# A matrix product in fp16 on one core: w's blocks converted two at a time, and the first group's differences made for two blocks in one operation

## The chip, the cores and the metric

The kernel runs on one core of a Trainium2 chip. The metric is the device time of one execution in microseconds (us), as the median of several runs. The engines are called by their short names: PE (TensorE, matrix products), DVE (VectorE), ACT (ScalarE), POOL (GpSimd) and SP (SyncE, whose queue issues the DMAs).

## The reference

```python
cs = np.cumsum(x, axis=1)
diff = cs - np.concatenate([zeros, cs[:, :-1, :]], axis=1)
return np.matmul(diff, w).astype(np.float32)
```

x is 8 x 2048 x 2048 and w is 2048 x 2048, both float32. The differences of the running sums are x itself, so that the kernel computes x times w, with x as 16384 rows of 2048. On the chip that is 128 tiles of 128 rows.

## The kernel before

**Products.** Four row tiles make a group: g, g+1, g+2 and g+3, of which the code calls g+2 "h". The kernel splits the 2048 contraction values and the 2048 columns in two each, so that w has four blocks B11, B12, B21, B22, and pairs of row tiles are combined in a scheme with seven products in place of eight. For that it needs four differences of w's blocks: T1 = B12 - B11, T2 = B22 - T1, T3 = B22 - B12, T4 = B21 - T2. Blocks and differences are fp16, scaled by one number for each column half of w, made from sums of absolute values (`uw`, and its reciprocal `uinv`). Row tiles are scaled too: ACT measures a tile (`weigh`), DVE makes its scale (`scale_of`, two tiny operations), POOL its unit for the way back (`unit_of`), ACT narrows it to fp16 (`narrow`), and SP issues two transposing DMAs (`turn`). Results leave PSUM scaled by the unit, by ACT (`keep`, the first part of an output) or DVE (`add`, a further part), and SP stores them (`put`).

**The storage of w.** `W_all` holds w as it was loaded, float32, in eight slots k of 4 x 1024 values. The two halves of the contraction (a) and of the columns (h) each take 1024 float32 values of a slot, 4096 bytes. A converted block takes half of that place, as two runs of 512 fp16 values with a gap of 512 after each, and the difference of the same place takes the gaps:

```python
blocks = W_all.bitcast(f16).rearrange("p k (i n j c) -> p i j k n c", i=4, j=2, c=NB)

def spare_of(i, k):
    return blocks[:, i // 2, i % 2, ds(k, 2), :, :]
```

With i from 0 to 7 these are B11, T1, B12, T2, B21, T3, B22, T4. A conversion (`block`, lines 337 to 346; DVE's form at 341, ACT's at 345) multiplies the 1024 float32 values of one slot by `uinv` and writes them in place. `spare_of(i, k)` is the view of two slots, k and k+1, of one of the eight; it is used before the change for sums inside later groups.

**The head.** The first four row tiles are multiplied plainly in bf16 while w is loaded, in two passes over w's column halves (h = 0 and 1) of 16 steps ko, eight matmuls a step in the second pass. Each step has `cast` (DVE writes the bf16 copy `wb`, line 266) and `measure` (ACT, line 272). In the second pass `bring(ko)` fetches, casts and measures step ko, and then converts one block of the first half with `turn_left(1)`, in the order B11 0 to 7, B21 0 to 7, from ko = 1. At ko = 10 it loads and measures tile 4, and DVE makes its scale. The matmuls of steps 0 to 11 go over all four rows; those of steps 12 to 15 are done row by row by `finish_row(r)`, which then copies the row's two PSUM banks out (ACT the even bank, DVE the odd, lines 331 and 333). After the last step come `greatest_of_w(1)` and `scale_of_w(1)` (the scale of the second half, with a reduction on POOL), the one block left (`turn_left(KH)`), and then the eight blocks of B12, with the rows' copies among them. `left_over` (line 457) is a product of 16 matmuls that the first pass left out; it reads B11 and B21. Then the head makes T1 (line 506), eight operations.

**The first group** (`group_plain`, tiles 4 to 7). It converts B22 (0 to 5 on ACT, 6 and 7 on DVE) and makes T2, T3 and T4 with `lessen` (line 586), one slot at a time, each ahead of the product that reads it. Products of sixteen matmuls with 512 columns (line 604) read a block k after k. Its first sums of row tiles (`total`, line 594) need the transposes of tile 5.

**What sets the order.** Each engine works in the order of the program: `after(engine, ...)` ties each operation behind the last one of its engine, and SP's DMAs likewise. Waits between engines come from the data. From the second group (`group_half`) on, the order is a list of steps written out by hand, which this change does not touch.

Of the kernel before, what the change touches and what calls it, by code (L numbers as in the profile page):

```python
# [10 lines left out]
def kernel(  # L11
# [6 lines left out]
    nc = tc.nc  # L18
    P = 128
    B, S, D = x.shape  # L20
# [4 lines left out]
    KH = KO // 2  # L25
    NH = N // 2
    NB = 512
# [4 lines left out]
    SUB = mybir.AluOpType.subtract  # L32
    MUL = mybir.AluOpType.mult
# [18 lines left out]
    W_all = const.tile([P, KH, 4 * NH], f32, name="W")  # L52
# [5 lines left out]
    B11, T1, B12, T2, B21, T3, B22, T4 = (  # L58
        [p[:, i // 2, i % 2] for p in pieces] for i in range(8)
    )  # L60
# [6 lines left out]

    def spare_of(i, k):
        return blocks[:, i // 2, i % 2, ds(k, 2), :, :]

    uw = const.tile([P, 2], f32, name="uw")
    uinv = const.tile([P, 2], f32, name="uinv")
# [9 lines left out]
    def bank(i):  # L82
        return psum.tile([P, NB], f32, name=f"b{i}")
# [3 lines left out]
    def after(engine, ask):  # L87
        if engine in last:
            with tc.issue_after(last[engine].ins):
                said = ask()  # L90
        else:
            said = ask()
        last[engine] = said[-1] if isinstance(said, tuple) else said
        return said
# [90 lines left out]
    with ExitStack() as head:  # L185
# [70 lines left out]
        def fetch(h, ko):  # L256
            wt = whole[ko % KH][:, ko // KH, h, :]
            nc.sync.dma_start(wt, w[ds(ko * P, P), ds(h * NH, NH)])
# [37 lines left out]
        def here(h, r):  # L296
            return range(1 if h == 0 and r == PLAIN - 1 else 2)
# [39 lines left out]
        def block(dst, a, h, k, engine):  # L337
            src = whole[k][:, a, h, :].rearrange("p (n c) -> p n c", c=NB)
            if engine == "dve":
                after(  # L340
                    "dve", lambda: nc.vector.tensor_scalar(dst[k], src, uinv[:, h : h + 1], None, MUL)  # L341
                )
            else:
                after(
                    "act", lambda: nc.scalar.activation(dst[k], src, COPY, scale=uinv[:, h : h + 1])
                )

        def dummies(banks):
            for i in banks:
                after(  # L350
                    "pe",
                    lambda: nc.tensor.matmul(
                        bank(i), zeros[:, :P], zeros, start=True, stop=True
                    ),
                )
# [25 lines left out]
        for ko in range(1, KO - 2):  # L381
# [3 lines left out]
            q = (ko + 1) // KQ  # L385
# [3 lines left out]
            for r in range(PLAIN):  # L389
                if turning and r in (0, PLAIN - 1):  # L390
                    a = r // 2
# [13 lines left out]
        for ko in range(AHEAD):  # L405
            measure(1, ko)
        ps = [[bank(2 * r + n) for n in here(1, r)] for r in range(PLAIN)]
        left = [(B, a, k) for a, B in enumerate((B11, B21)) for k in range(KH)]

        def turn_left(n):  # L410
            for _ in range(min(n, len(left))):
                B, a, k = left.pop(0)
                block(B, a, 0, k, "dve")

        def bring(ko):
            fetch(1, ko)
            cast(1, ko)
            measure(1, ko)
            if ko == AHEAD:
                scale_of_w(0)  # L420
            turn_left(1)
            if ko == 10:
                load(PLAIN, 0)
                load(PLAIN, 1)
                weigh(PLAIN)
                scale_of(PLAIN)
            if ko == 11:
                narrow(PLAIN)
# [18 lines left out]
        def finish_row(r):  # L447
            for ko in range(KO - KQ, KO):
                plain(1, r, ko)
            plain_out(1, r)  # L450
# [16 lines left out]
            rows = ds((PLAIN - 1) * P, P)  # L467
            after("sp", lambda: put(c, rows, ds(NB, NB), nc.sync))

        turn_left(KH)  # L470
        unit_of(PLAIN)
        turn(PLAIN)
        weigh(PLAIN + 2)
        finish_row(0)
        for k in range(KH):
            block(B12, 0, 1, k, "dve")
            if k == 1:
                scale_of(PLAIN + 2)
            if k % 2:
                if k // 2:  # L480
                    finish_row(k // 2)
        unit_of(PLAIN + 2)
        narrow(PLAIN + 2)
        there = xP.rearrange("p r k m -> p (r k m)")
# [17 lines left out]
        stores(done[:3] + done[5:])  # L502
        left_over(bank(2))

        for k in range(KH):
            after("dve", lambda: nc.vector.tensor_tensor(T1[k], B12[k], B11[k], SUB))


    class Part:
# [64 lines left out]
    def in_twos(t):  # L574
        return t if len(t.shape) == 4 else t.rearrange("p (a b) n -> p a b n", b=2)
# [4 lines left out]

    def half_of(t, i):
        return in_twos(t)[:, i]

    def lessen(dst, p, q):
        for k in range(len(dst)):
            after("dve", lambda: nc.vector.tensor_tensor(dst[k], p[k], q[k], SUB))

    def less(dst, p, q):
        if len(dst.shape) == 4 or len(p.shape) == 4 or len(q.shape) == 4:
# [88 lines left out]
    def group_plain(g, X, Y, Z, V):  # L678
        h = g + 2
        lg, lh, kg = (units(t)[0] for t in (g, h, g + 1))  # L680
        ug, uh, vg = (units(t)[1] for t in (g, h, g + 1))
        A11g, A12g = parts(g)
        A11h, A12h = parts(h)
        A21g, A22g = parts(g + 1)
        A21h, A22h = parts(h + 1)
        S1g, S1h = S1
        S2g, S2h, S3g, S3h, S4g, S4h = A11g, A11h, A21g, A21h, A12g, A12h
        load(g + 4, 0)
        load(g + 4, 1)
        product(X, A11g, B11, True)  # L690
        for k in range(3):
            block(B22, 1, 1, k, "act")
        C11g = pair()
        keeps(C11g, X, lg)
        weigh(h + 1)
        for k in range(3, KH):
            block(B22, 1, 1, k, "act" if k < 6 else "dve")
        product(V, A12g, B21, True)
        product(Y, A11h, B11, True)
        lessen(T2[:1], B22[:1], T1[:1])  # L700
        adds(C11g, V, lg)
        puts(C11g, g, 0)
        lessen(T2[1:2], B22[1:2], T1[1:2])
        total(S1g, A21g, A22g, ADD)
        total(S3g, A11g, A21g, SUB)
        total(S2g, S1g, A11g, SUB)
        scale_of(h + 1)
        unit_of(h + 1)
        narrow(h + 1)
        kh, vh = units(h + 1)  # L710
        turn(h + 1)
        lessen(T2[2:], B22[2:], T1[2:])
        product(Z, A12h, B21, True)
        C11h, C22g = (
            [
                inner[:, ds(j, 2), :].rearrange("p a n -> p (a n)").bitcast(f32)
                for j in (i, i + 2)
            ]
            for i in (12, 16)
        )  # L720
        keeps(C11h, Y, lh)
        product(V, S1g, T1, True)
        keeps(C22g, V, vg)
        load(h + 4, 0)
        total(S4g, A12g, S2g, SUB)
        product(X, S2g, T2, False)
        C12g = pair()
        keeps(C12g, X, ug)
        lessen(T3, B22, B12)
        product(V, S4g, B22, False)  # L730
        total(S1h, A21h, A22h, ADD)
        total(S3h, A11h, A21h, SUB)
        total(S2h, S1h, A11h, SUB)
        weigh(g + 4)
        scale_of(g + 4)
        unit_of(g + 4)
        narrow(g + 4)
        load(h + 4, 1)
        turn(g + 4)
        load(g + 5, 0)  # L740
        load(g + 5, 1)
        product(X, S3g, T3, False)
        adds(C11h, Z, lh)
        puts(C11h, h, 0)
        del free[-2:]
        adds(C12g, V, ug)
        puts(C12g, g, 1)
        product(Y, S2h, T2, False)
        C12h = pair()
        keeps(C12h, Y, uh)  # L750
        adds(C22g, X, vg)
        puts(C22g, g + 1, 1)
        del free[-2:]
        total(S4h, A12h, S2h, SUB)
        product(Z, S1h, T1, True)
        weigh(h + 4)
        lessen(T4[:4], B21[:4], T2[:4])
        scale_of(h + 4)
        unit_of(h + 4)
        lessen(T4[4:], B21[4:], T2[4:])  # L760
        C22h = pair()
        keeps(C22h, Z, vh)
        narrow(h + 4)
        weigh(g + 5)
        product(Y, S3h, T3, False)
        in_2.first()
        in_2.fourth()
        load(h + 5, 0)
        load(h + 5, 1)
        turn(h + 4, [0])  # L770
        scale_of(g + 5)
        unit_of(g + 5)
        adds(C22h, Y, vh)
        puts(C22h, h + 1, 1)
        product(Z, S4h, B22, False)
        in_2.third()
        adds(C12h, Z, uh)
        puts(C12h, h, 1)
        narrow(g + 5)
        weigh(h + 5)  # L780
        turn(h + 4, [1])
        turn(g + 5, [0])
        product(X, A22g, T4, False)
        C21 = pair()
        keeps(C21, X, kg)
        puts(C21, g + 1, 0)
        turn(g + 5, [1])
        product(Y, A22h, T4, False)
        less(in_3.Q1, in_3.t12, in_3.t11)
        scale_of(h + 5)  # L790
        unit_of(h + 5)
        C21 = pair()
        keeps(C21, Y, kh)
        narrow(h + 5)
        in_3.second()
        less(in_1.Q1, in_1.t12, in_1.t11)
        turn(h + 5)
        load(g + 8, 0)
        load(g + 8, 1)
        puts(C21, h + 1, 0)  # L800
# [462 lines left out]
    for b in range(-early, len(groups) - late):  # L1263
        for name, ahead in ORDER:
            i = b + ahead
# [41 lines left out]
```

## Time and profile before

| | |
|---|---|
| median of 3 runs | 1451.99 us (1451.88 to 1452.24) |
| the profiled execution's own time | 1450.92 us |
| its span in the trace | 1449.10 us |
| granted clock of TensorE | 1.00 throughout |
| busy: PE, DVE, ACT, POOL | 1439.1, 1318.3, 971.7, 43.5 us |
| conversions on DVE (line 341) | 26, from 42.0 to 79.6 us, median 750 ns |
| T1 on DVE (line 506) | 8, from 74.2 to 78.4 us, median 686 ns |
| T2, T3 and T4 on DVE (line 586) | 24, from 80.3 to 108.8 us, median 686 ns |
| PE's left-over product | starts at 68.03 us |
| the first group's first product | starts at 71.48 us |

Times in the text are microseconds from the start of the span unless something else is said. A timeline row has the start, the length, the engine, the line of the kernel, the operation, what it writes and reads by the program's names, shapes, how many neighbours were merged into the row, and in brackets the idle time of the engine before it with what ended it. The chain of work that ended last is followed back from the last instruction, at each step to what released it. The durations of matmuls include the pipeline, so that the distance between starts is what counts for PE.

### The profile page before, as it was taken

To read this page: it belongs to the slowest core of one execution; us is meant where nothing else is said; L and a number is where in the kernel's file an instruction comes from. 1 tells how busy PE (TensorE), PEld (TensorE's weight loads), DVE (VectorE), ACT (ScalarE), POOL (GpSimd) and SP (SyncE) were. 2 spreads that over 40 slices of the span, in tenths; PEclk is the share of its full clock that TensorE was granted. 3 is DMA by queue.
4 is the path that set the end of the run, shared out by engine and by line. 5 is a ranking of instruction groups with operands and counts; after the bars stand their busy time and mean duration, and the time that the engine had idled before them with its cause. 6 is when DMAs were issued, how large, how long until landed. Compare 5 with 4: busy or idle time off the path is not lost.

```text
span 1449.1 us, 20194 instructions
## 1 busy us (share of the span) xinstructions
PE 1439.1 (99%) x6686; PEld 651.7 (45%) x6692; DVE 1318.3 (91%) x2309; ACT 971.7 (67%) x1473; POOL 43.5 (3%) x130
## 2 busy tenths in 40 slices
PE   8999999999999999999999999999999999999998
PEld 4444444444444444444444444444444444444443
DVE  5898899999999999999999999999999999999998
ACT  6987567766666776666666667666667766666662
POOL 0011000000000000000000000000000000000000
PEclk9999999999999999999999999999999999999999
DMA  9999788899888898888898878998878998889973
GB/s 363 371 246 294 202 232 237 234 258 246 231 220 241 243 248 243 231 234 239 248 250 232 235 232 235 263 236 237 228 234 239 253 239 235 224 244 247 254 201 126
DMA packets 378199, 351.58 MB, mean 243 GB/s; under 512 B 274800, under 2 KB 274800, under 8 KB 377968
## 3 DMA queue, kind: packets, MB, share of 16 engines
q1 hardware_dynamic: 378096, 350.31, 86.7%
q8 instruction: 52, 0.85, 0.2%
q14 instruction: 51, 0.42, 0.1%
HBM read 150.99 MB, written 134.22 MB: 197 GB/s over the span
## 4 chain that ended last, share of the span: by engine, by line
PE 93%; DMA 5%; DVE 1%; issue 0%; ACT 0%; SPq 0%; DVEq 0%; ACTq 0%
PE b L623 61%; PE b L604 31%; DMA W<-in_w_dram 4%; DMA x<-F 1%; DVE c L634 1%; PE b L303 0%; DVE x L594 0%; PE b L457 0%; DMA out_dram<-c 0%; DVE wb L266 0%; DVE W L341 0%; ACT c L631 0%; ACT F L163 0%; SPq L224 0%; DVE S L594 0%
## 5 line engine op out<-in xcount | busy, mean ns | idle before, releaser
L634 DVE SCALAR_TENSOR_TENSOR c<-b,of,c 128x512 f32<-128x512 f32 x790 | 573.6, 746 | 70.2 <-PE b L623 60.0
L604 PE MATMUL b<-W,x 128*128 128x512 f16 x2144 | 506.8, 379 | 0.2 <-DVE x L594 0.2
L631 ACT ACTIVATE c<-b,of 128x512 f32<-128x512 f32 x492 | 312.7, 680 | 223.0 <-PE b L623 117.2
L623 PE MATMUL b<-W,x 128*128 128x512 f16 x1904 | 455.0, 379 | 0.1
L163 ACT ACTIVATE F<-F,of 128x1024 f16<-128x1024 f32 x246 | 282.2, 1147 | 175.1 <-DVE of L143 172.9
L623 PEld LDWEIGHTS <-x 128*128 128x128 f16 x2500 | 244.6, 98 | 296.1 <-issue 1.9
L604 PEld LDWEIGHTS <-x 128*128 128x128 f16 x2144 | 209.7, 98 | 253.4 <-DVE x L594 0.7
L124 ACT ACTIVATE waste<-F 128x1024 uint8<-128x1024 f32 x246 | 259.3, 1054 | 8.7 <-DMA F<-in_x_dram 6.6
L623 PEld LDWEIGHTS <-inner 128*128 128x128 f16 x1644 | 160.9, 98 | 194.0 <-issue 0.2
L623 PE MATMUL b<-W,inner 128*128 128x512 f16 x940 | 241.2, 379 | 0.0
L594 DVE TENSOR_TENSOR x<-x,x 128x1024 f16<-128x1024 f16 (+1 forms) x390 | 227.2, 583 | 3.2
L623 PE MATMUL b<-flow,x 128*128 128x512 f16 x588 | 150.9, 379 | 0.1
L623 PE MATMUL b<-inner 128*128 128x512 f16 x472 | 121.1, 379 | 0.0
L947 DVE TENSOR_TENSOR flow<-W 128x2048 f16<-128x2048 f16 x88 | 107.0, 1216 | 0.0
L1040 DVE TENSOR_TENSOR b<-b,c 128x512 f32<-128x512 f32 x116 | 80.5, 694 | 13.4 <-PE b L623 13.4
L149 POOL TENSOR_SCALAR of<-uw,of 128x2 f32<-128x2 f32 x124 | 42.2, 354 | 1301.6 <-DVE of L141 719.3
L947 DVE TENSOR_TENSOR flow<-W,inner 128x2048 f16<-128x2048 f16 x58 | 70.8, 1220 | 0.0
L1033 ACT COPY c<-b 128x512 f32<-128x512 f32 x58 | 33.4, 576 | 52.1 <-PE b L623 46.6
L303 PE MATMUL b<-wb,xP 128*128 128x512 bf16 x234 | 53.5, 379 | 2.8 <-ACT wb L264 1.9
L594 DVE TENSOR_TENSOR inner<-x 128x512 f16<-128x512 f16 x117 | 49.3, 421 | 3.1 <-DMA x<-F 1.1
L1033 ACT COPY b<-b 128x512 f32<-128x512 f32 x87 | 51.2, 588 | 0.0
L594 DVE TENSOR_TENSOR inner<-x,inner 128x512 f16<-128x512 f16 x117 | 49.2, 421 | 2.0
(66 smaller groups left out, 516.6 us busy)
## 6 DMA issues: line engine op xcount, KB each, us to landing
F<-in_x_dram SPq DMA_DIRECT2D x246, 512.0 KB, 5.3
out_dram<-c SPq DMA_DIRECT2D x492, 256.0 KB, 3.1
W<-in_w_dram SPq DMA_DIRECT2D x32, 512.0 KB, 8.4
W<-in_x_dram SPq DMA_DIRECT2D x16, 256.0 KB, 7.8
x<-F SPq DMA_TRANSPOSE x246, 3.4
out_dram<-o SPq DMA_DIRECT2D x5, 256.0 KB, 7.6
out_dram<-wb SPq DMA_DIRECT2D x5, 256.0 KB, 3.5
xP<-in_x_dram SPq DMA_DIRECT2D x1, 1024.0 KB, 6.2
```

Of the source, the lines that this page charges most:

```text
L124: lambda: nc.scalar.activation(waste, where[t][i], ABS, scale=1.0 / ROW, accum_out=sums_of[t][:, i : i + 1],),
L149: after("pool", lambda: nc.gpsimd.tensor_scalar(u, uw, m, None, MUL))
L163: lambda: nc.scalar.activation(narrowed(t)[:, ds(i * NH, NH)], where[t][i], COPY, scale=s),
L303: lambda: nc.tensor.matmul(ps[r][n], xP[:, r, ko, :], wb[h, ko][:, ds(n * NB, NB)], start=(ko == 0), stop=(ko == KO - 1),),
L594: after("dve", lambda: nc.vector.tensor_tensor(dst.all, p.all, q.all, op))
L604: said = nc.tensor.matmul(to[n], a[k], b[k][:, n, :], start=(first and k == 0), stop=(k == KH - 1), skip_group_check=True,)
L623: said = nc.tensor.matmul(to, a[k], b[k], start=(first and k == 0), stop=(k == 3), skip_group_check=True)
L631: after("act", lambda: nc.scalar.activation(c, p, COPY, scale=u))
L634: after("dve", lambda: nc.vector.scalar_tensor_tensor(c, p, u, c, MUL, ADD))
L947: after("dve", lambda: nc.vector.tensor_tensor(in_twos(flow), x, y, op))
L1033: after("act", lambda: nc.scalar.copy(c, p))
L1040: after("dve", lambda: nc.vector.tensor_tensor(t, p, s, ADD))
```

## The change

Two helpers come in. `two_blocks(i, a, h, k)` converts slots k and k+1 of one block in one DVE operation; `minus(to, i, j, ks)` makes a difference for two slots in one DVE operation.

```diff
+    def minus(to, i, j, ks):
+        for k in ks:
+            a, b, c = (spare_of(n, k) for n in (to, i, j))
+            after("dve", lambda: nc.vector.tensor_tensor(a, b, c, SUB))
...
+        def two_blocks(i, a, h, k):
+            src = W_all[:, ds(k, 2), ds((2 * a + h) * NH, NH)]
+            src = src.rearrange("p k (n c) -> p k n c", c=NB)
+            after(
+                "dve",
+                lambda: nc.vector.tensor_scalar(
+                    spare_of(i, k), src, uinv[:, h : h + 1], None, MUL
+                ),
+            )
...
-        left = [(B, a, k) for a, B in enumerate((B11, B21)) for k in range(KH)]
+        left = [(4 * a, a, 0, k) for a in range(2) for k in range(0, KH, 2)]
...
-            turn_left(1)
+            if ko % 2 == 0:
+                two_blocks(*left.pop(0))
...
-        turn_left(KH)
+        two_blocks(*left.pop(0))
...
-        for k in range(KH):
-            block(B12, 0, 1, k, "dve")
-            if k == 1:
+        for k in range(0, KH, 2):
+            two_blocks(2, 0, 1, k)
+            if k == 0:
                 scale_of(PLAIN + 2)
-            if k % 2:
-                if k // 2:
-                    finish_row(k // 2)
+            else:
+                finish_row(k // 2)
...
-        for k in range(KH):
-            after("dve", lambda: nc.vector.tensor_tensor(T1[k], B12[k], B11[k], SUB))
+        minus(1, 2, 0, range(0, KH, 2))
...
-        for k in range(3, KH):
-            block(B22, 1, 1, k, "act" if k < 6 else "dve")
+        for k in range(3, 6):
+            block(B22, 1, 1, k, "act")
+        two_blocks(6, 1, 1, 6)
...
-        lessen(T2[:1], B22[:1], T1[:1])
+        minus(3, 6, 1, (0,))
         adds(C11g, V, lg)
         puts(C11g, g, 0)
-        lessen(T2[1:2], B22[1:2], T1[1:2])
...
-        lessen(T2[2:], B22[2:], T1[2:])
+        minus(3, 6, 1, (2, 4, 6))
...
-        lessen(T3, B22, B12)
+        minus(5, 6, 2, range(0, KH, 2))
...
-        lessen(T4[:4], B21[:4], T2[:4])
+        minus(7, 4, 3, (0, 2))
         scale_of(h + 4)
         unit_of(h + 4)
-        lessen(T4[4:], B21[4:], T2[4:])
+        minus(7, 4, 3, (4, 6))
```

In `bring` the conversions stand at the even steps ko = 2 to 14, and the eighth pair of the first half comes where the one left-over block came. Row copies, scales and units keep their places among the conversions of B12. In the first group the difference of T2's second slot moves ahead of the two adds of C11g. The conversions on ACT stay single.

More of the change, by code (lines that the diff above doesn't have):

```diff
@@ L407 @@
         ps = [[bank(2 * r + n) for n in here(1, r)] for r in range(PLAIN)]
-        left = [(B, a, k) for a, B in enumerate((B11, B21)) for k in range(KH)]
[L410 to L413, printed above, removed]
+        left = [(4 * a, a, 0, k) for a in range(2) for k in range(0, KH, 2)]
         def bring(ko):
@@ L468, in left_over @@
             after("sp", lambda: put(c, rows, ds(NB, NB), nc.sync))
-        turn_left(KH)
+        two_blocks(*left.pop(0))
+        assert not left
         unit_of(PLAIN)
@@ L582, in half_of @@
         return in_twos(t)[:, i]
-    def lessen(dst, p, q):
-        for k in range(len(dst)):
-            after("dve", lambda: nc.vector.tensor_tensor(dst[k], p[k], q[k], SUB))
     def less(dst, p, q):
```

## The prediction

> **What bounds the kernel now.** I read the page's busy table first, then the waits of TensorE, the chain of work that ended last, and the timelines of the engines from 36 to 150 us, the only stretch that the diff touches.
>
> ```profile
> PE 1439.1 (99%) x6686; PEld 651.7 (45%) x6692; DVE 1318.3 (91%) x2309; ACT 971.7 (67%) x1473; POOL 43.5 (3%) x130
> PE 93%; DMA 5%; DVE 1%; issue 0%; ACT 0%; SPq 0%; DVEq 0%; ACTq 0%
> 200.89 18.13 PE b L623 x84
> ```
>
> TensorE (PE) fills the span and makes 93% of the chain; VectorE (DVE), 91% busy, makes 1%. The third line, from the chain, gives PE's pace: 18.13 us / 84 = 0.2158 us a matmul. The number of matmuls does not change, so the time changes only where PE stands still. Where PE stands still is counted from its timeline, starts against the pace:
>
> ```profile
> 71.48 13.98 PE L604 MATMUL b<-W,x 128*128 128x512 f16 x64
> 85.35 3.63 PE L604 MATMUL b<-W,S 128*128 128x512 f16 x16
> 88.82 10.52 PE L604 MATMUL b<-W,x 128*128 128x512 f16 x48
> 99.50 3.63 PE L604 MATMUL b<-W,x 128*128 128x512 f16 x16 [0.16 <-DVE x L594]
> ...
> 134.09 1.89 PE L604 MATMUL b<-W,x 128*128 128x512 f16 x8
> 136.12 1.02 PE L623 MATMUL b<-flow,x 128*128 128x512 f16 x4
> ```
>
> 64 matmuls from 71.48 should end at 85.29, and the next starts at 85.35: 0.06 lost. 48 from 88.82 should end at 99.18; the next starts at 99.50: 0.32 lost. 8 from 134.09 should end at 135.82; the next starts at 136.12: 0.30 lost. These three, 0.68 us, are nearly all that PE loses from 42 to 142 us; read in the same way, some 0.5 more goes in small pieces up to 191, and then next to nothing. So **no saving on DVE can bring more than about 1.2 us**, 0.08%. The question is what the change can make late.
>
> **Prices.** These rows of DVE's timeline carry them:
>
> ```profile
> 61.02 0.75 DVE L341 TENSOR_SCALAR W<-W,uinv 128x1024 f16<-128x1024 f32 x1
> 61.68 0.69 DVE L266 CAST wb<-W 128x1024 bf16<-128x1024 f32 x1
> 62.28 0.75 DVE L341 TENSOR_SCALAR W<-W,uinv 128x1024 f16<-128x1024 f32 x1
> 64.28 0.17 DVE L287 TENSOR_REDUCE wtop<-wsum 128x1 f32<-128x16 f32 x1 [1.25 <-ACT waste L272]
> ...
> 65.20 0.73 DVE L341 TENSOR_SCALAR W<-W,uinv 128x1024 f16<-128x1024 f32 x1
> 65.85 0.69 DVE L333 COPY wb<-b 128x512 f32<-128x512 f32 x1
> ...
> 69.41 0.69 DVE L333 COPY x<-b 128x512 f32<-128x512 f32 x1
> ...
> 74.18 4.89 DVE L506 TENSOR_TENSOR W<-W 128x1024 f16<-128x1024 f16 x8
> ...
> 124.28 1.22 DVE L591 TENSOR_TENSOR W<-W,inner 128x2048 f16<-128x2048 f16 x1
> 125.42 1.22 DVE L591 TENSOR_TENSOR W<-W 128x2048 f16<-128x2048 f16 x1
> ```
>
> Neighbours overlap a little, so I count from start to start. A single conversion holds DVE 0.66 us (61.02 to 61.68), a cast 0.60 (61.68 to 62.28). Single differences hold it (4.89 - 0.69) / 7 = 0.60 each. A difference of twice the size is in the trace, with the same two-block shape: 124.28 to 125.42 is 1.14. A pair of differences so saves 1.20 - 1.14 = 0.06, and sixteen of them (T1 to T4) about 1.0 us. A pair of conversions is not in the trace; I call what it holds DVE p. Its 1024 more elements cost 1.14 - 0.60 = 0.54 in the differences, which run at the same 1024 elements in 0.6 us; that gives an estimate of **p = 1.20**. No saving would be p = 1.32. The upper bound is one element at a time: the copies from PSUM at 65.85 take 0.69 for 512 elements where the cast takes 0.69 for 1024, so the doubled work could take 4 x 0.53 + 0.12 = 2.25. I take 1.20, the nearest row by size and rate. 13 pairs in place of 26 singles then save 1.6 us. In all DVE saves 2.6 us of its 1318.
>
> **Part 1: the seven pairs beside the second pass over w** (`bring`). The single conversions at ko = 1 to 14 become pairs at ko = 2, 4 ... 14; the one at ko = 15 goes. Queued behind a pair are the casts of wb, and PE waits for those. The last cast, ko = 15, is the tight one. PE comes to 16 matmuls of the leftover product at 68.03, so the pass of 128 began at 68.03 - 128 x 0.2158 = 40.41, and its 103rd matmul, the first that needs wb of ko = 15, is due at 62.42. The cast ends at 61.68 + 0.69 = 62.37. From the last wait of DVE before it (for ACT's measure of tile 4, to 56.29) there are now five casts and two pairs in place of five casts and four singles, so the cast moves by 2p - 2.64: 0.24 earlier by my p, later than due only from p = 1.35. The wait to 56.29 itself is ACT's; DVE stood idle 2.2 us ahead of it, which covers the pairs before. The other casts come no later than now. Gain on PE: nothing, as it was on time.
>
> **Part 2: the last pair of B21, and B12.** Here something is lost. The single at 62.28 used idle time ahead of the wait to 64.28. Its block now goes with the last one, as a pair at 65.20, after that wait: 9 singles (5.9 us) become 5 pairs (6.0) between 65.20 and 74.18, and what stands among them moves by: the copy of bank 1 at 65.85 p - 0.66 = +0.54; the copy of bank 3 at 69.41 3p - 5 x 0.66 = +0.30; the copy of bank 7 and scale_of of tile 5 at 73.85 5p - 9 x 0.66 = +0.06. PE needs banks 0 and 1 at 71.48 and bank 7 at 71.48 + 16 x 0.2158 = 74.93; the copy of bank 7 now ends at 73.94, so 0.99 is spare. What is not spare is SP's queue:
>
> ```profile
> 70.12 1.16 SPq L313 DMA_DIRECT2D out_dram<-x  x2
> 71.39 4.20 SPq L176 DMA_TRANSPOSE x<-F  x2
> 75.64 1.05 SPq L112 DMA_DIRECT2D F<-in_x_dram  x2
> 76.80 5.72 SPq L176 DMA_TRANSPOSE x<-xP  x2
> ```
>
> SP stands from 67.1 until the copy of bank 3 is done (70.10) to store it; behind that store are the transposes of tile 6, two loads and the transposes of tile 5. DVE waits for the last (idle 1.67 to 84.60), makes S1g from them, and PE's product at 85.35 follows S1g at once. So +0.30 at bank 3 can be +0.30 on PE. Against it: the DMA engines are busy 0.9 or more of each us from 70 to 73 with stores issued before, and landings run to 75.7, so a later issue may only shorten the backlog. Bounds 0 and +0.30; I take the middle, **+0.15**. The later stall at 99.50 hangs on the same queue (stores, then tile 7's transposes), so it moves along with the first and adds nothing.
>
> **Part 3: B22 and the differences.** T1 ends 0.2 earlier, the pair of B22 0.3. T2's second block now stands ahead of the two adds at 80.93, which come some 0.1 later; their stores are issued only at 88.21, and bank V is asked for at 85.35. Of T2 PE reads block k at 88.82 + 0.43k; its last pairs end near 88.2, 89.3 and 90.5, in time for 89.68, 90.55 (blocks 4, 5) and 91.4. T3 is due from 95.7 and its pairs end by 95.8 with block 6 due at 98.3; T4 is due after 109. All hidden by PE's own work. After 99.50 the waits are for transposes that PE itself releases, so what is saved on DVE is waited away.
>
> **Sum.** The profiled execution took 1450.92 (span 1449.10 and 1.82 around it): 1450.92 + 0.15 = 1451.07. The median of the runs is 1.07 higher, 1451.99, so **1452.1**.
>
> **Rivals.**
> 1. *The pair runs at half rate* (p = 2.25): slower. The place is the cast of ko = 15, the point p = 1.35. By 2.25 the wait to 56.29 is passed 2.3 late, the cast ends near 66.5, PE is 4.1 late; scale_of of tile 5 comes 2.2 + 5 x 2.25 - 5.9 = 7.5 late, and ACT's narrowing, the transposes and S1g behind it. 1451.99 + 7.5 = 1459.5. For: no row of such a form. Against: the single conversion already writes two separated runs and holds 1024 elements in 0.66. Chance 0.08. The Trainium skill (VectorE: DVE Perf Modes, What auto-detection actually checks) says that one-source operations keep two elements a cycle when the outermost sizes of both sides are even or equal; here that size is 2 on both sides, so by the page p stays near 1.2.
> 2. *The units come late.* POOL's three unit operations stand from 74.70 to 77.93 beside T1, where one alone at 99.67 takes 0.29. If they get through only when DVE rests (82.9), ACT's first scaling of C11g waits from 80.22 for 2.7, B22's last blocks and the narrowing of tile 7 with it; its transposes, due at 90.99, wait for a narrowing that ends at 92.1: +1.1, 1453.1. Against: they got through between singles, about two DVE operations each; between pairs that is 2.3 us each, ends near 76, 78 and 80.5, and first uses are at 80.22, 89.34 and 90.48. Chance 0.04. The Trainium skill (SBUF — State Buffer, Who interferes with whom) calls the pair of ports that VectorE and GpSimd share an exclusive lock held for the whole instruction; the stretched POOL rows agree, and by it longer operations hold longer, which speaks against this change.
> 3. *The stalls shrink.* If an earlier DVE feeds 85.35, 99.50 and 136.12 sooner: -0.68, 1451.3. For: DVE is named at 99.50. Against: ahead of it DVE is idle for a transpose (1.14 to 97.23). Chance 0.10.
> 4. *Not done as said*: pairs split into the old instructions. 1452.0; the counts would tell. Chance 0.02.
>
> My forecast has 0.74; 0.02 is left for what I have not seen.
>
> **Range and chances.** 0.2% (2.9 us) is about what a measurement of this kernel can tell from no change. Forecast, units, stalls and no-change all lie within it: 0.90 less the unseen. The low end is rival 3 less the runs' spread of 0.36: 1450.9. The high end takes in p = 1.32 (+0.66 at bank 3 and scale_of), rival 2 and a p up to about 1.5 (5 x 1.5 - 5.9 = +1.6): 1453.7. Rival 1 stays out. Faster 0.02, same 0.89, slower 0.09.
>
> **What would show it.** Conversions: 13 rows of 128x2048 near 1.27 long, 1.20 apart; if 2.3, rival 1. Cast of ko = 15 ends near 62.1. The copy of bank 3 starts near 69.7 and tile 6's transposes are issued near 71.7. PE's start near 85.35 shows the 0 to 0.3. POOL's three end by 80.5. I am wrong if PE shows a new gap at 62.4 or 74.9, or one after 100 that is not there now.

## The result and the profile after

The changed kernel takes 1454.2 us (22 runs, 1452.9 to 1455.7), the kernel before 1452.2 in 22 runs beside them (1451.0 to 1452.9). The ratio is **1.0014** (95% interval 1.0008 to 1.0020): slower by 2.0 us, where some 0.15 was forecast, and past the upper end of the range, 1453.7. The profiled execution of the changed kernel took 1453.01 with a span of 1451.1, 2.0 more than before's span; 0.34 of that had come before any changed operation: uinv's first reciprocal ends at 42.28 in place of 41.94. It ends anywhere from 41.94 to 42.48 in the traces of this document, whose kernels all do the same up to there. From here on the times of the changed kernel's trace are its own, 0.34 included. Lines of code have moved: 258 is now 263 (a load of w), 266 is 271 (the cast of wb), 341 is 358 (conversions), 506 and 586 are 74 (differences), 303, 604 and 623 are 308, 610 and 629 (PE's matmuls).

The page's busy table and the chain's shares by engine, after:

```profile
PE 1439.3 (99%) x6686; PEld 651.6 (45%) x6692; DVE 1316.1 (91%) x2280; ACT 971.5 (67%) x1473; POOL 45.4 (3%) x130
PE 91%; DMA 5%; ACT 2%; DVE 1%; issue 1%; SPq 0%; DVEq 0%; POOL 0%; ACTq 0%
```

DVE does less (1316.1 for 1318.3 us, 29 instructions fewer) and PE's work is the same, but PE's share of the chain falls from 93 to 91% and ACT enters with 2%. PE's timeline, after:

```profile
63.35 5.77 PE L308 MATMUL b<-wb,xP 128*128 128x512 bf16 x25 [0.65 <-DVE wb L271]
...
72.42 14.15 PE L610 MATMUL b<-W,x 128*128 128x512 f16 x64
86.44 3.63 PE L610 MATMUL b<-W,S 128*128 128x512 f16 x16
89.91 10.57 PE L610 MATMUL b<-W,x 128*128 128x512 f16 x48
100.74 3.63 PE L610 MATMUL b<-W,x 128*128 128x512 f16 x16 [0.26 <-DVE x L600]
...
135.47 1.89 PE L610 MATMUL b<-W,x 128*128 128x512 f16 x8
137.51 1.02 PE L629 MATMUL b<-flow,x 128*128 128x512 f16 x4
```

There is a gap of 0.65 at 63.35, for a cast of wb: the place that the prediction called tight. It is larger than before, but not wholly new. PE's loads of its weights (PEld), one for each matmul, show it best. Before, after, and in the run with the pairs in one slot (below), which has no gap there:

```profile
62.42 1.60 PEld L303 LDWEIGHTS <-xP 128*128 128x128 bf16 x8 [0.34 <-issue]
63.35 0.53 PEld L308 LDWEIGHTS <-xP 128*128 128x128 bf16 x3 [0.93 <-issue]
60.01 3.98 PEld L308 LDWEIGHTS <-xP 128*128 128x128 bf16 x19
```

A weight load that is not held starts 0.2158 behind the last one and takes 0.10, so 0.12 of such a gap is usual: PE loses 0.22 there before and 0.81 after. By the pace of 0.2158, 0.21 is lost up to 86.44 (0.06 before), 0.47 up to 100.74 (0.32), 0.20 at 132.02 (0.05 at 130.64) and 0.31 up to 137.51 (0.30). One more wait, 0.69 for ACT near 167, makes up the rest in this execution; such a wait was also there, and longer, in a run without any loss (the pairs in one slot), so it is not put down to the change. DVE's timeline leads to the cause:

```profile
42.82 1.29 DVE L358 TENSOR_SCALAR W<-W,uinv 128x2048 f16<-128x2048 f32 x1
44.02 1.29 DVE L271 CAST wb<-W 128x1024 bf16<-128x1024 f32 x2
...
52.48 0.69 DVE L271 CAST wb<-W 128x1024 bf16<-128x1024 f32 x1 [0.57 <-DMA W<-in_w_dram]
...
56.88 0.21 DVE L146 TENSOR_SCALAR of<-of 128x1 f32<-128x1 f32 x1 [2.52 <-ACT waste L129]
...
58.25 0.69 DVE L271 CAST wb<-W 128x1024 bf16<-128x1024 f32 x1 [0.34 <-DMA W<-in_w_dram]
...
61.42 1.28 DVE L358 TENSOR_SCALAR W<-W,uinv 128x2048 f16<-128x2048 f32 x1
62.61 0.69 DVE L271 CAST wb<-W 128x1024 bf16<-128x1024 f32 x1
...
65.86 1.27 DVE L358 TENSOR_SCALAR W<-W,uinv 128x2048 f16<-128x2048 f32 x1
...
70.34 0.69 DVE L338 COPY x<-b 128x512 f32<-128x512 f32 x1
...
76.10 0.21 DVE L146 TENSOR_SCALAR of<-of 128x1 f32<-128x1 f32 x1 [1.35 <-ACT waste L129]
...
76.42 4.61 DVE L74 TENSOR_TENSOR W<-W 128x2048 f16<-128x2048 f16 x4
```

A pair holds DVE 44.02 - 42.82 = 1.20 us, as estimated. But casts now wait for loads of w (52.48, 58.25), which they did not before in this stretch. SP's timeline says why. Before:

```profile
33.87 7.04 SPq L258 DMA_DIRECT2D W<-in_w_dram  x7
41.86 1.60 SPq L112 DMA_DIRECT2D F<-in_x_dram  x2
44.46 5.37 SPq L258 DMA_DIRECT2D W<-in_w_dram  x5
...
58.51 6.21 SPq L176 DMA_TRANSPOSE x<-F  x2
```

and after, with the first line of its waits of SP from 36 to 75 (who waited for whom: total, times, longest):

```profile
33.84 13.02 SPq L263 DMA_DIRECT2D W<-in_w_dram  x8
46.90 0.95 SPq L117 DMA_DIRECT2D F<-in_x_dram  x2
47.90 4.26 SPq L263 DMA_DIRECT2D W<-in_w_dram  x5
...
60.78 6.19 SPq L181 DMA_TRANSPOSE x<-F  x2
```

```profile
SPq L263 <- DVE W L358: 9.2, 4, 5.7
```

The loads that came between 33.9 and 40.9 now last to 46.9. Four of them wait for DVE's pairs, 9.2 us in all, the longest 5.7. They are the loads of w for ko = 8, 10, 12 and 14. The trace has them issued at 44.13, 46.53, 48.93 and 51.34, each 0.03 behind the end of a pair (44.10, 46.50, 48.91, 51.31). The listing of SP's instructions in the program as built, with the semaphores that they wait for, has the waits. DMAHW0 to DMAHW7 stand for earlier DMAs: there are eight, taken in turn, so that a DMA waits for the landing of the eighth before it, and at most eight are under way. DVE stands for a count of DVE's operations. These are the loads of ko = 8, 9 and 10 after; before, the same three have no wait for DVE:

```
37 L263 DMACopy W_58<-in_w_dram 128x1024 [waits DMAHW0_49,DVE_49]
38 L263 DMACopy W_58<-in_w_dram 128x1024 [waits DMAHW1_49]
39 L263 DMACopy W_58<-in_w_dram 128x1024 [waits DMAHW2_49,DVE_49]
```

The load of ko = 8 + k fills slot k's last quarter. A pair of slots k and k+1 reads and writes the first quarter (B11) or the third (B21) of both: not one byte of the load's. But from its first byte to its last the pair's span runs over the end of slot k, and the program as built treats the two as touching. The odd loads do not wait: slot k+1's end lies past the span.

### The profile page after: what moved, and what is told of

It reads as the page before. It is cut to its first block, busy times and chain, and to the rows that moved or that the text cites. A ratio compares the mean times of both kernels' runs of the same rounds, so it can differ in the third digit from the quotient of the medians.

```text
span 1451.1 us, 20171 instructions
## 1 busy us (share of the span) xinstructions
PE 1439.3 (99%) x6686; PEld 651.6 (45%) x6692; DVE 1316.1 (91%) x2280; ACT 971.5 (67%) x1473; POOL 45.4 (3%) x130
## 4 chain that ended last, share of the span: by engine, by line
PE 91%; DMA 5%; ACT 2%; DVE 1%; issue 1%; SPq 0%; DVEq 0%; POOL 0%; ACTq 0%
PE b L629 61%; PE b L610 30%; DMA W<-in_w_dram 3%; DMA x<-F 1%; DVE c L640 1%; DMA xP<-in_x_dram 0%; DVE x L600 0%; ACT waste L277 0%; DMA out_dram<-x 0%; PE b L308 0%; ACT F L168 0%; DMA out_dram<-c 0%; ACT W L350 0%; DMA out_dram<-wb 0%; ACT c L637 0%
```

## The experiments

The theory (**A** in the texts): the whole loss is these waits, which make the loads late. The rivals: the differences in pairs (B), the pairs themselves (C), the eighth pair left over behind the scale's wait (D). All times stand beside runs of the kernel before on the same chip; "GB/s" is what the DMA engines moved from 46 to 56 us, from the table by stage. With these numbers of runs the intervals are about 0.09% wide to each side, 1.3 us. The ratios follow the means (within 0.0002) and not the medians: of the 11 runs of the differences only, for one, eight lie between 1451.0 and 1451.7 and three between 1453.3 and 1454.0, so its median is 0.7 under before's while its mean, 1451.9, is 0.1 under. A difference of the medians of under a microsecond is therefore not read as a gain.

| run | median | before | ratio (95%) | GB/s |
|---|---|---|---|---|
| the change | 1454.2 | 1452.2 | 1.0014 (1.0008 to 1.0020) | 334 |
| first half single | 1452.1 | 1452.0 | 1.0000 (0.9991 to 1.0009) | 410 |
| first half in pairs, no more | 1453.8 | 1452.0 | 1.0012 (1.0004 to 1.0021) | 345 |
| the waits alone | 1453.8 | 1452.0 | 1.0014 (1.0005 to 1.0022) | 338 |
| pairs in one slot | 1451.6 | 1452.0 | 1.0001 (0.9992 to 1.0010) | 408 |
| differences only | 1451.4 | 1452.1 | 1.0000 (0.9991 to 1.0008) | 409 |
| one slot, odd steps | 1451.7 | 1452.1 | 1.0000 (0.9991 to 1.0009) | 408 |
| wait at load 8 alone | 1454.4 | 1452.1 | 1.0018 (1.0010 to 1.0027) | 352 |
| waits at loads 12 and 14 | 1451.8 | 1452.1 | 0.9999 (0.9990 to 1.0008) | 407 |
| shorter wait at load 8 | 1453.2 | 1451.6 | 1.0012 (1.0004 to 1.0021) | 392 |
| wait at load 10 alone | 1454.9 | 1451.6 | 1.0022 (1.0012 to 1.0032) | 315 |

**The first half single.** The changed kernel with `left`, `turn_left` and its calls as before; the five pairs of B12 and B22 and all paired differences stay.

```diff
...
-            if ko % 2 == 0:
-                two_blocks(*left.pop(0))
+            turn_left(1)
...
-        two_blocks(*left.pop(0))
-        assert not left
+        turn_left(KH)
```

> The changed kernel with the sixteen conversions of B11 and B21 single again, at the places that they had before; the pairs of B12 and B22 and all paired differences stay. Theory A (a pair's two slots count as one stretch up to the other slot, so that SP's loads of w for ko = 8, 10, 12 and 14 wait for DVE's pairs, and all loads behind them come some 2 us late): the waits are gone, the load of ko = 8 is issued near 38 us and not at 44, PE's gap near 62.3 is gone, and the time is that of before within 0.5 us (1451.7 to 1452.7). Rival B (the paired differences, or T2's second block ahead of the adds, cost it): still some 2 us over before, 1454. Rival C (a pair of conversions costs by itself, wherever it stands): 5 of 13 pairs are left, so 0.6 to 0.8 over before.

1.0000: the loss is gone. Rival B falls, and C with it as far as the interval reaches (0.8 over before would lie inside it). One part of the expectation did not hold in the profiled execution: its loads still landed 1.1 late (load 15 lands 13.9 behind load 7 in place of 12.8), because 2.4 us passed between two landings near 48 with no wait of SP for DVE. PE then stands 1.14 at 86.80, for sums of tile 5. Nothing here explains that gap between the landings.

**The first half in pairs, no more.** The kernel before with the eight pairs of B11 and B21 alone.

```diff
-            turn_left(1)
+            if ko % 2 == 0:
+                two_blocks(*left.pop(0))
...
-        turn_left(KH)
+        two_blocks(*left.pop(0))
```

> The kernel before with only the conversions of B11 and B21 in pairs, as the change has them; B12, B22 and all differences stay single. Theory A: the whole loss is here, 1.3 to 2.2 us over before, with the load of ko = 8 issued near 44 us, the cast of ko = 15 near 62.6 and a gap of 0.6 in PE at 62.3. Rival B: within 0.3 of before. Rival C: 1.2 over before.

1.0012: as A has it. The load of ko = 8 is issued at 44.31.

**The waits alone.** The kernel before, every operation single. DVE writes two values a partition, ahead of their being overwritten by the load, at the places that the even loads will fill; each write takes 0.06 us.

```diff
             turn_left(1)
+            if ko in (2, 4, 6, 8):
+                after("dve", lambda: nc.vector.memset(whole[ko - 2][:, 1, 1, :2], 0.0))
```

> The kernel before, all operations single; after the conversions at ko = 2, 4, 6 and 8 DVE writes two values into the place that the load of w for ko = 8, 10, 12 and 14 will fill, so that the load has to wait for DVE where the change makes it wait, and nothing is paired. Theory A: 1.3 to 2.2 us over before, as the wait alone makes the loss, with loads issued at 44.1, 46.6, 49.1 and 51.6 us. Rivals B and C, and rival D (the last block moved from idle time behind the scale's wait): within 0.3 of before.

1.0014, the ratio of the change itself, without a pair in the kernel. Its SP timeline shows the same picture:

```profile
33.92 13.03 SPq L258 DMA_DIRECT2D W<-in_w_dram  x7
46.99 0.96 SPq L112 DMA_DIRECT2D F<-in_x_dram  x2
47.99 4.75 SPq L258 DMA_DIRECT2D W<-in_w_dram  x5
```

This run separates A from B, C and D: the waits are enough. (The writes themselves cost nothing that can be measured: two of them stand in a run below that loses nothing.)

**The pairs in one slot.** The changed kernel, but a pair is B11 and B21 of one slot. The span ends at the third quarter's end, ahead of what the load fills.

```diff
-        left = [(4 * a, a, 0, k) for a in range(2) for k in range(0, KH, 2)]
+        left = list(range(KH))
+
+        def both_blocks(k):
+            src = whole[k][:, :, 0, :].rearrange("p a (n c) -> p a n c", c=NB)
+            after(
+                "dve",
+                lambda: nc.vector.tensor_scalar(
+                    pieces[k][:, 0:4:2, 0], src, uinv[:, :1], None, MUL
+                ),
+            )
...
-                two_blocks(*left.pop(0))
+                both_blocks(left.pop(0))
...
-        two_blocks(*left.pop(0))
+        both_blocks(left.pop(0))
```

> The changed kernel, with the eight pairs of the first half made of B11 and B21 of one slot in place of two slots of one block: the same number, size and places of operations on DVE, but the stretch that a pair spans ends ahead of the place that the loads of ko = 8 to 15 fill. Theory A: no wait at the loads, and the time of before within 0.5 us. Rivals B, C and D: all of their causes are still there, so some 2 us over before, 1454.

1.0001. DVE does the same number of pairs of the same size at the same steps, the eighth left over as in the change, and the loss is gone. With that D falls too. Its SP timeline is that of before:

```profile
33.90 7.42 SPq L263 DMA_DIRECT2D W<-in_w_dram  x8
42.27 1.61 SPq L117 DMA_DIRECT2D F<-in_x_dram  x2
44.83 5.55 SPq L263 DMA_DIRECT2D W<-in_w_dram  x5
```

**The differences only.** The kernel before with `minus` in place of `lessen` and of T1's loop, nothing else.

> The kernel before with only T1 to T4 made for two slots at a time, T2's second slot ahead of the adds; every conversion single. The prediction held these to be hidden: within 0.4 us of before (some 1452.0), PE's gaps at 85 and 99 as before. A theory in which the differences' wider spans make waits too would give 0.5 or more over before.

1.0000. The differences are hidden, as the prediction had them.

**Pairs in one slot at the odd steps.** As the pairs in one slot, but at ko = 1, 3 ... 15, so that none is left over. Against that run:

```diff
-            if ko % 2 == 0:
+            if ko % 2:
                 both_blocks(left.pop(0))
...
-        both_blocks(left.pop(0))
         assert not left
```

> The changed kernel with pairs of B11 and B21 of one slot, at the odd steps 1 to 15, so that the eighth stands in the idle time ahead of the second half's scale and nothing is left behind it. Theory A: no wait at the loads; DVE from the scale on does 8 conversions' work less 0.66, so that the copy of bank 3 comes some 0.9 earlier than in the pairs of one slot before, and the time is that of before or 0.1 to 0.6 under it (1451.4 to 1452.0). If the bound is PE alone, no difference can be measured.

1.0000. In its profile the gaps near 62, 85 and 100 are gone, but others have come: PE stands at 44.38 for the cast behind the first pair (0.26 idle, 0.42 by the pace) and loses 0.24 at 131. So no gain can be measured. No version that beats the kernel before was found.

**Which wait costs.** Two runs with a part of the writes: at ko = 2 only, and at ko = 6 and 8 only.

> The kernel before with the one write at ko = 2, so that only the load for ko = 8 (and SP's queue behind it) waits, to 44.1 us in place of 38.0. Theory A in its finer form (a late issue costs only as far as the eight loads under way run down): three are left at 44.1, the load of 8 lands near 48.8 in place of 48.2, the later ones 0.4 to 0.8 late, and the time is 0.2 to 0.7 over before. If every wait cost alike, a quarter to a half of the 1.8.

> The kernel before with the writes at ko = 6 and 8 only, so that the loads for ko = 12 and 14 wait, some 3.4 us each at SP. Finer form of theory A: at 49.1 us five loads are still under way, nothing runs down, the loads land as before (55.9 and 58.5 us by the clock of before) and the time is that of before within 0.3. If every wait cost alike, some 0.9 over before.

The second came out as expected: SP stands 5.0 us for DVE and it costs nothing (0.9999), since the loads issued earlier are still coming in. In its SP timeline the five later loads are spread over 8 us, and the load of ko = 15 lands 12.9 us behind that of ko = 7, as before (12.8):

```profile
42.04 1.60 SPq L112 DMA_DIRECT2D F<-in_x_dram  x2
44.62 7.99 SPq L258 DMA_DIRECT2D W<-in_w_dram  x5
```

The first was a miss in size: 0.2 to 0.7 us expected, 1.0018 (2.3 us) measured, as much as all four waits within the intervals. The loads came 1.2 late and not 0.4 to 0.8 (load 15 lands 14.0 behind load 7). Two more runs try the edge: one write behind the first conversion, so that load 8 is issued about a microsecond earlier than in the first, and one at ko = 4, for load 10 alone. The first of them, against the waits alone:

```diff
-            if ko in (2, 4, 6, 8):
-                after("dve", lambda: nc.vector.memset(whole[ko - 2][:, 1, 1, :2], 0.0))
+            if ko == 1:
+                after("dve", lambda: nc.vector.memset(whole[ko - 1][:, 1, 1, :2], 0.0))
```

> The kernel before with one write, behind the first conversion (ko = 1), so that the load for ko = 8 is issued near 42.8 us in place of 38.0 (44.3 in the run with the wait at load 8 alone). At 42.8 four loads are under way, the last to land at 46.9; a load lands 4.8 us after its issue when few are ahead of it, so that of ko = 8 lands near 47.6 to 48.2, as before. If the loss comes from the loads under way running down, later loads land as before and the time is that of before within 0.5. If any wait in front of load 8 costs 2 us, 1454.

> The kernel before with one write, at ko = 4, so that only the load for ko = 10 waits, to 46.6 us in place of 40.6, and what is behind it. Three loads are left under way (46.9, 48.2, 49.5), as in the run with the wait at load 8 alone, so the load of 10 and all after it should land about 1.2 late, as there, and the time be 1 to 2.3 over before. If only load 8 matters, the time of before.

The shorter wait was expected to be free and was not: 1.0012 (1.0004 to 1.0021). Its load 8 landed in time (48.72), but loads 9 and 10 came 1.7 and 1.5 us after one another in place of 1.28, and load 15 0.6 late. The wait at load 10 alone cost 1.0022, so it is not load 8 that matters. In size this was a miss too: 3.3 us, where 1 to 2.3 were expected, and load 15 lands 2.8 late and not 1.2. Of the 2.8, 1.0 arises at load 8, which had been issued in time and lands 2.3 behind load 7, with load 9 alone behind it until SP goes on at 46.8.

What fits these runs is how many loads are under way when SP goes on: with three (loads 8 and 10) or four (the shorter wait) there is a loss, with five (loads 12 and 14) there is none. That is argued from one execution of each and is not a sharp rule: load 10 of the shorter wait was issued with five under way and still landed 1.5 behind load 9.

What the table by stage shows of the DMA engines, from 46 to 56 us (columns: length, busy time of PE, PEld, DVE, ACT and POOL with the number of instructions, granted clock, share of the DMA engines, GB/s). Before:

```profile
46.00:56.00 10.00, 9.95 (x47) 4.57 (x47) 8.11 (x13) 9.75 (x17) 0.00 (x0) 1.00 1.03 409
```

after:

```profile
46.00:56.00 10.00, 9.95 (x47) 4.53 (x47) 7.80 (x10) 9.50 (x17) 0.00 (x0) 1.00 0.96 334
```

the waits alone:

```profile
46.00:56.00 10.00, 9.95 (x48) 4.52 (x47) 8.21 (x16) 9.04 (x17) 0.00 (x0) 1.00 0.95 338
```

and the pairs in one slot:

```profile
46.00:56.00 10.00, 9.95 (x47) 4.58 (x47) 7.75 (x10) 9.72 (x18) 0.00 (x0) 1.00 1.03 408
```

75 GB/s less for 10 us is 0.75 MB that did not come, 1.8 us of loading at 409. Every run with under 400 in this row is slower, every run with over 400 is not (one execution of each).

## Why the prediction was wrong

**The step that failed** is one sentence of part 1: "Queued behind a pair are the casts of wb, and PE waits for those." It looked at what stands behind the pair in DVE's own queue and not at who waits for the pair itself. SP's loads of w do, and the prediction does not name them in this stretch: it put their lateness at nothing without a reason. With it fell the next steps, "The other casts come no later than now" (the casts of ko = 10 and 12 wait for their loads) and "Gain on PE: nothing". Nothing in the diff names a load, and no load's bytes are touched; the wait arises because an operation over two slots spans what lies between them. The trace of before could not show it: no two-slot operation of DVE stood ahead of a load of w there.

**From the waits to PE.** SP issues in order, so the load of ko = 8, held 5.7 us, holds everything behind it: seven loads of w, tile 4's and tile 6's rows, the stores, and the load of tile 5. Before the hold, each load landed 1.28 us behind the last (512 KB at 410 GB/s); once the loads under way have run down, the next four landings (loads 8, 9 and 10 and the first half of tile 4) come 1.70, 1.26, 2.19 and 1.95 behind one another, and from then on 1.25 to 1.29 again, so that the delay stays. The load of ko = 15 comes 14.8 us behind that of ko = 7 in place of 12.8. The Trainium skill (DMA: Bandwidth & Descriptors, Anatomy of one DMA — SWDGE (gpsimd) path) says that any semaphore wait of a DMA is made by the sequencer that issues it, and that the DMA engines only work off their queues. The trace agrees: it is SP that stands, 5.7 us, and the engines that then have less to do (0.96 busy for 1.03). Then two paths lead to PE, and the chain of after shows pieces of both:

```profile
47.90 8.97 DMA W<-in_w_dram
...
60.23 1.14 ACT waste L277 x2
61.42 0.63 DVE W L358
62.05 0.57 issue
62.61 0.70 DVE wb L271
63.35 1.67 PE b L308 x7
65.08 1.99 PE b L308 x9
67.06 6.65 DMA xP<-in_x_dram
73.73 1.16 ACT waste L129 x2
74.92 1.16 ACT waste L129 x2
76.10 0.22 DVE of L146
76.34 0.17 DVE of L148
76.54 1.16 ACT xP L168
```

First the cast of ko = 15: the load of ko = 14 lands at 60.72, its cast, the pair and the last cast follow, and the last one ends at 63.30 in place of 62.37; PE, itself 0.35 later here, stands 0.65. The chain reaches this pair (61.42) through ACT's measurement of load 12. That is the span once more: load 12 fills a place between the pair's two slots, and DVE has a wait for ACT there that it has not before. It decided nothing here, since the pair starts 0.61 behind the cast ahead of it, as the pair at 58.86 does.

Then tile 5. The first transpose of tile 4 waits for the landing of load 14, the eighth DMA before it, and is issued at 60.78 in place of 58.51; behind the two transposes comes the load of tile 5, at 67.06 in place of 64.81. (The chain names PE ahead of it; on SP it stands 0.09 behind the transposes in both kernels.) It lands at 73.71 in place of 71.02, ACT measures it, DVE's scale of tile 5 starts at 76.10 (73.85 before; DVE stands 1.35 for it), ACT narrows, and the transposes and S1g follow, for PE's product at 86.44.

**The rest, point by point.**
- PE bounds, and no saving on DVE can bring more than some 1.2 us: held. Saving DVE's work without the waits gave 1.0000 and 1.0001. The list of PE's losses lacks one, though: 0.22 at 62.42, for the cast of ko = 15. The prediction reckoned the time at which that cast is due back from 68.03, and so found it on time, when PE was waiting for it already.
- p = 1.20: measured 1.20 (1.28 long, over the 13 pairs a median of 1281 ns). A pair of differences holds DVE (4.61 - 1.22) / 3 = 1.13 us for the 1.14 taken.
- Part 1's sum for the cast of ko = 15, 0.24 earlier: it holds where the loads are in time. In the run with pairs in one slot the cast ends 5.82 behind DVE's scale of tile 4 in place of 6.08, 0.26 earlier, and PE stands for no cast there: a gain of 0.2 on PE where nothing was forecast.
- The copy of bank 3 was to move by +0.30 against the first conversion behind uinv's second value: from 65.20 and 69.41 to 65.86 and 70.34, +0.27. It was priced right. Counted for +0.15 on PE it can't be told from nothing in the time: the run with all of it and without the waits lies at 1.0001. In that run's profile PE loses 0.24 up to 85.72, 0.18 more than before, about what was forecast; the gain at the cast makes up for it.
- scale_of of tile 5 at +0.06: measured +1.6 by the same clock, 1.35 of it DVE's wait for the late load.
- Part 3, the differences: held (1.0000).
- Rival 1, half rate: did not happen. It named a right place (the cast of ko = 15) with a wrong mechanism, and its price of 7.5 us was not needed: in the profiled execution 0.6 came from the place that it named, and a few tenths from the later stalls.
- Rival 2, the units: beside pairs of differences a unit of POOL's takes two of DVE's operations, as foreseen, and nobody waits for it. After the change this met one of the three, the other two being through at 73.1; with the differences only it met all three, to 79.93, at a ratio of 1.0000.

```profile
76.41 2.43 POOL L154 TENSOR_SCALAR of<-uw,of 128x2 f32<-128x2 f32 x1 [3.33 <-DVE of L146]
```

- Rival 3, the stalls shrink: seen at 85 and 100 only in the run at odd steps, where others came in their place.
- The chances: 0.89 for no change by 0.2%, and the ratio is 1.0014. A change clear of the noise had not been forecast, and the range was too short, 1453.7 for 1454.2. That the forecast lay on the slower side, by 0.15 for bank 3, is no credit: the loss came from elsewhere. And 0.2% was not what a measurement can tell: 22 runs of each gave 0.06% to each side.

What stays open: where the lost 2.0 us fall on PE differs from execution to execution. In the profiled one of the waits alone they lie at 63, 80, 88 and 102 us of its own clock, in that of the wait at load 8 mainly at 100 and 132, with a little at 86, and a single profile does not settle the split (the place near 132 loses as much, 0.40, in the differences only, at no cost in the time); the profiled executions of the change (1453.01) and of the wait at load 8 (1452.13) are also among the quickest of their kernels, 1.2 and 2.2 under the medians, so their gaps show where time is lost and not the whole of the loss. Why a queue of three or four loads moves less than one of eight was not tried by itself.

## What to carry to other kernels

Before two operations are merged into one, list who waits for each of them and what each must wait for, in every queue; a merged operation over strided places may be taken to span all that lies between, and a load into a gap then waits although no byte is shared. Merge along the dimension whose span stays clear of places that transfers still have to fill (here the two blocks of one slot), and compare the waits in the built program's listing. In these runs a wait in a queue that works ahead cost nothing while five transfers were still under way, and made everything behind it late once they had run down to three or four: count what is under way at the moment of the late issue.

## What was not expected of the hardware

- Eight loads of 512 KB under way land 1.28 us apart (410 GB/s). With three or four left at the moment of the next issue, two or three of the following landings are 1.5 to 2.7 us apart, and the time is not made up: in the ten microseconds from 46 the engines moved 315 to 392 GB/s in place of 407 to 410. A wait of 3.4 us with five under way cost nothing (0.9999).
- A POOL operation on 128x2 values takes 0.29 us alone, 1.19 to 1.37 beside DVE's differences of 0.69 us and 2.43 beside those of 1.22: in both cases up to two of DVE's operations.
